# The last 448 columns of unit 28's store leave in two transfers of 123 and 5 rows

## The chip, the cores and the metric

The kernel runs on one core of one Trainium2 chip. The metric is device time in microseconds (us) of one execution, as the median of several runs. The core has TensorE (PE in the profile), VectorE (DVE), ScalarE (ACT), GpSimd (POOL) and SyncE (SP), and 16 DMA engines that carry all traffic between HBM and the on-chip memory SBUF.

## The reference

The input is `logits` of shape (32, 128, 4 heads, 4096) and `prior` of shape (32, 128, 4), both float32. Every head's row of 4096 logits goes through a softmax, the four prior values through another, and the output is the mixture of the four heads:

```
prior_probs = softmax(prior, axis=-1)                  # (32, 128, 4)
probs = softmax(logits, axis=-1)                       # (32, 128, 4, 4096)
out = sum over heads of prior_probs[..., None] * probs # (32, 128, 4096) float32
```

The logits are 268.4 MB and the output is 67.1 MB.

## The kernel before, in words

A **unit** is one of the 32 batches: 128 rows on the 128 partitions, four heads of 4096 columns each. A head of a unit is a tile of 128x4096 float32, 16 KB in each partition. The tile `ring` holds 12 of these in SBUF (L87); `place` (L101) says which of the twelve slots a head gets, so that a slot serves three units on.

The operations, one letter each in the order that is written out by hand (L26 to L60):

- `L` is `load` (L110 to L116): one transfer for a run of heads whose slots are neighbours, from `nc.sync`, that is SP.
- `M` is `peak` (L122): the negative row maximum, on VectorE. `E` is `exp` (L127): exponential and row sum on ScalarE. `R` is `recip` (L133).
- `G` is `diagonal` (L136): a 128x128 diagonal matrix of prior over row sum, on GpSimd. `X` is `weigh` (L143): TensorE multiplies by it and accumulates heads 0 to 2 in PSUM (`acc`), 512 columns an instruction.
- `C` is `weight`, `Z` is `scale`, and `A`, `B`, `T`, `V`, `P` and `W` bring head 3 and the sum in PSUM together, on VectorE (L163), or over ScalarE (L182) and GpSimd (L157, L179, L185). The result of a unit stands in the slot of its head 3, which the kernel calls `home` (L107).
- `S` is `store` (L118 to L120): it sends the result, or a stretch of its four 1024-column quarters, to HBM. Units 2 to 21 leave on ScalarE's queue, all others on SP's.

`digits` behind a letter are the head and the quarters, and `@u` is the unit. An engine runs its instructions strictly in the order in which the list gives them to it. SP therefore issues loads and stores in one row: a store whose data aren't ready holds up each load behind it.

The change concerns the end of SP's row. The last loads are those of unit 31 (`L01@31`, `L12@31`, `L23@31`, `L34@31`, one head each). Behind them SP has only stores: `S@28`, `S@29`, `S@30`, each of 128 rows of 16 KB (2048 KB), and then the four quarters of unit 31, `S23@31`, `S34@31`, `S01@31` and `S12@31`, each of 128 rows of 4 KB (512 KB). No load waits for any of these.

A transfer lies in the trace as packets, one for each row, with a start, a duration and a size, and at its end one packet of 4 bytes from each DMA engine that took part, which counts up the transfer's completion semaphore.

Of the kernel before, what the change touches and what calls it, by code (L numbers as in the profile page):

```python
# [67 lines left out]
def kernel(  # L68
# [7 lines left out]
    U, P, H, V = logits.shape  # L76
# [27 lines left out]
    def slot(u, h, a=0, b=4):  # L104
        return ring[:, place(u, h), a * C : b * C]

    def home(u, a, b):  # L107
        return slot(u, 3, a, b)
# [8 lines left out]

    def store(u, a=0, b=4):  # L118
        queue = nc.scalar if 2 <= u < 22 else nc.sync
        queue.dma_start(out=out[u, :, a * C : b * C], in_=home(u, a, b))  # L120

    def peak(u, h):  # L122
# [61 lines left out]
    def add_scaled(u, a, b):  # L184
        nc.gpsimd.tensor_add(home(u, a, b), slot(u, 1, a, b), slot(u, 3, a, b))  # L185

    step = {
        "L": load, "S": store, "M": peak, "E": exp, "R": recip, "G": diagonal, "X": weigh,
        "C": weight, "Z": scale, "A": add_last, "B": add_head, "T": add_both, "V": evac,
        "P": add_scaled, "W": add_second,  # L190
# [11 lines left out]
    with tc.manual_schedule():  # L202
# [6 lines left out]
            out=ident, in_=ident, pattern=[[-1, P]], compare_op=ALU.is_equal, fill=0.0,  # L209
# [48 lines left out]
```

## Time and profile before

| what | value |
| --- | --- |
| median of 3 runs | 787.11 us (786.59 to 787.41) |
| the profiled execution's own time | 787.09 us |
| its span, first to last instruction | 785.4 us |
| TensorE busy, share of the span | 681.8 us, 87% |
| VectorE busy | 645.1 us, 82% |
| ScalarE busy | 547.5 us, 70% |
| GpSimd busy | 293.8 us, 37% |
| moved by DMA | 335.90 MB, mean 428 GB/s |
| last instruction of VectorE (L163) starts, ends | 778.39, 779.67 us |
| `S@28`, `S@29`, `S@30` issued | 735.53, 753.93, 770.09 us |
| the four quarters of unit 31 issued | 775.15, 776.31, 777.50, 779.70 us |

The profiled execution's time is 1.69 us above its span: that is what lies around the instructions. The page of the profile gives totals, 40 slices of the span, the DMA queues and the chain of work that ended last; the view by windows gives the same shares for stretches that one chooses; the timeline gives single instructions; and the trace holds each DMA packet, without saying which of the 16 engines carried it. Queue q1 is SP's and q10 is ScalarE's; q8 and q14 carry instructions.

### The profile page before, as it was taken

The page shows a single profiled execution, that of the slowest core. Times are in us where ns is not written, and L with a number is a line of the kernel's source. Part 1 is how long each engine was busy: PE and PEld are TensorE (multiplying, and loading weights), DVE is VectorE, ACT ScalarE, POOL GpSimd, SP SyncE. Part 2 cuts the span into 40 slices and gives each one's busy share as a digit, 9 for nine tenths or more (in the row PEclk, how much of TensorE's full clock was granted, in tenths as well). Part 3 has the DMA queues.
Part 4 walks back from the last instruction along what each step waited for, and adds up shares of the span by engine and source line. Part 5 has one row for each costly group of instructions (what it writes and reads, how often), then busy time and mean ns, then how long its engine had stood idle before and what let it go on. Part 6 is the DMA issues. An engine that isn't in the chain of part 4 may idle for free.

```text
span 785.4 us, 4589 instructions
## 1 busy us (share of the span) xinstructions
PE 681.8 (87%) x1508; PEld 293.0 (37%) x1508; DVE 645.1 (82%) x327; ACT 547.5 (70%) x326; POOL 293.8 (37%) x243
## 2 busy tenths in 40 slices
PE   0959998989999888998989989898888998899996
PEld 0424433333344333433334334343333443344342
DVE  6489977897778977779877798777888887979895
ACT  2557867867668666686676776766857668779883
POOL 0033323433134332334322343323430544277892
PEclk9989999999989999999999989999989899999999
DMA  9999999999999999999999999999999999999998
GB/s 378 456 411 426 429 436 413 433 437 441 435 416 431 448 436 421 434 424 436 444 429 430 420 436 438 439 427 421 432 449 421 440 408 431 451 412 431 429 429 351
DMA packets 15335, 335.90 MB, mean 428 GB/s; under 512 B 1712, under 2 KB 1712, under 8 KB 2256
## 3 DMA queue, kind: packets, MB, share of 16 engines
q1 hardware_dynamic: 12384, 293.61, 87.1%
q10 hardware_dynamic: 2928, 42.01, 12.5%
q8 instruction: 12, 0.20, 0.1%
q14 instruction: 11, 0.09, 0.0%
HBM read 268.50 MB, written 67.11 MB: 427 GB/s over the span
## 4 chain that ended last, share of the span: by engine, by line
DMA 58%; DVE 12%; PE 10%; POOL 10%; ACT 5%; issue 4%; SPq 0%; POOLq 0%; ACTq 0%
DMA ring<-in_logits_dram 58%; DVE nmax L123 11%; PE acc L146 10%; POOL ring L185 7%; ACT ring L128 3%; ACT ring L182 2%; POOL ring L179 1%; POOL ring L157 1%; POOL diag L137 1%; DVE ring L163 0%; SPq L115 0%; DVE rden L134 0%; SPq L120 0%; POOLq L185 0%; POOLq L137 0%
## 5 line engine op out<-in xcount | busy, mean ns | idle before, releaser
L146 PE MATMUL acc<-ring,diag 128*128 128x512 f32 x1508 | 681.8, 613 | 96.6 <-ACT ring L182 62.0
L123 DVE TENSOR_REDUCE nmax<-ring 128x1 f32<-128x4096 f32 x128 | 563.0, 4409 | 114.6 <-DMA ring<-in_logits_dram 114.6
L128 ACT ACTIVATE ring<-ring,nmax 128x4096 f32<-128x4096 f32 x128 | 474.6, 3708 | 202.5 <-DVE nmax L123 202.1
L146 PEld LDWEIGHTS acc<-ring,diag 128*128 128x128 f32 x1508 | 293.0, 196 | 484.5 <-issue 358.2
L185 POOL TENSOR_TENSOR ring<-ring 128x1024 f32<-128x1024 f32 x68 | 160.1, 2374 | 20.1 <-ACT ring L182 11.2
L137 POOL TENSOR_SCALAR diag<-ident,rden,pp 128x128 f32<-128x128 f32 x96 | 43.0, 448 | 239.7 <-DVE rden L134 239.7
L153 POOL TENSOR_TENSOR wght<-rden,pp 128x1 f32<-128x1 f32 x33 | 6.3, 190 | 210.4 <-DVE rden L134 210.4
L182 ACT ACTIVATE ring<-acc 128x1024 f32<-128x1024 f32 x68 | 66.7, 1012 | 17.9 <-PE acc L146 13.8
L157 POOL TENSOR_SCALAR ring<-ring,rden,pp 128x2048 f32<-128x2048 f32 (+3 forms) x35 | 74.2, 2121 | 9.0 <-DVE rden L134 8.7
L163 DVE SCALAR_TENSOR_TENSOR ring<-ring,wght,acc 128x1024 f32<-128x1024 f32 x60 | 74.2, 1269 | 3.3 <-PE acc L146 2.3
L134 DVE RECIPROCAL rden<-dsum 128x1 f32<-128x1 f32 x128 | 19.3, 153 | 10.2 <-ACT ring L128 10.2
L128 ACT ACTIVATION_READ_ACCUMULATOR ring<-ring,nmax 128x1 f32 x128 | 24.2, 189 | 0.0
L179 POOL TENSOR_TENSOR ring<-ring 128x1024 f32<-128x1024 f32 x5 | 11.8, 2367 | 0.1
L213 DVE TENSOR_REDUCE pmax<-pr 32x128 f32<-32x512 f32 x1 | 0.7, 674 | 5.3 <-DMA pr<-in_prior_dram 5.3
L215 ACT ACTIVATE pr<-pr 32x512 f32<-32x512 f32 x1 | 0.6, 628 | 4.2 <-DVE pr L214 4.2
L163 DVE SCALAR_TENSOR_TENSOR ring<-ring,wght 128x1024 f32<-128x1024 f32 x2 | 2.5, 1280 | 0.3 <-POOL wght L153 0.3
L215 ACT ACT_TABLE_LOAD x1 | 1.3, 1283 | 1.2 <-PEq L242 1.2
L222 DVE STREAM_TRANSPOSE pp<-pn 32x128 f32<-32x128 f32 x4 | 1.2, 302 | 0.1
L216 DVE TENSOR_REDUCE pmax<-pr 32x128 f32<-32x512 f32 x1 | 0.7, 674 | 0.7 <-ACT pr L215 0.7
L218 DVE TENSOR_TENSOR pn<-pr,pmax 32x512 f32<-32x512 f32 x1 | 1.0, 1016 | 0.0
L217 DVE RECIPROCAL pmax<-pmax 32x128 f32<-32x128 f32 x1 | 0.9, 941 | 0.0
L214 DVE TENSOR_TENSOR pr<-pr,pmax 32x512 f32<-32x512 f32 x1 | 0.7, 680 | 0.0
(6 smaller groups left out, 0.9 us busy)
## 6 DMA issues: line engine op xcount, KB each, us to landing
ring<-in_logits_dram SPq DMA_DIRECT2D x27, 6144.0 KB, 34.3
ring<-in_logits_dram SPq DMA_DIRECT2D x43, 2048.0 KB, 25.5
out_dram<-ring ACTq DMA_DIRECT2D x20, 2048.0 KB, 16.1
out_dram<-ring SPq DMA_DIRECT2D x11, 2048.0 KB, 14.0
out_dram<-ring SPq DMA_DIRECT2D x4, 512.0 KB, 5.5
pr<-in_prior_dram ACTq DMA_DIRECT2D x1, 64.0 KB, 4.5
ring<-in_logits_dram SPq DMA_DIRECT2D x1, 39.5
```

Source lines behind the costliest of these rows:

```text
L123: nc.vector.tensor_reduce(out=nmax[:, u, h : h + 1], in_=slot(u, h), op=ALU.max, axis=AX.X, negate=True)
L128: nc.scalar.activation(slot(u, h), slot(u, h), AF.Exp, bias=nmax[:, u, h : h + 1], accum_out=dsum[:, u, h : h + 1],)
L134: nc.vector.reciprocal(rden[:, u, h : h + 1], dsum[:, u, h : h + 1])
L137: nc.gpsimd.tensor_scalar(out=diag[:, u % 2, h], in0=ident, scalar1=rden[:, u, h : h + 1], scalar2=pp[:, h, u : u + 1], op0=ALU.mult, op1= ...
L146: nc.tensor.matmul(acc[:, k * W : (k + 1) * W], lhsT=diag[:, u % 2, h], rhs=e[:, k * W : (k + 1) * W], start=h == 0, stop=h == H - 2 or (u ...
L153: nc.gpsimd.tensor_mul(wght[:, u, h : h + 1], rden[:, u, h : h + 1], pp[:, h, u : u + 1])
L157: nc.gpsimd.tensor_scalar(out=e, in0=e, scalar1=rden[:, u, h : h + 1], scalar2=pp[:, h, u : u + 1], op0=ALU.mult, op1=ALU.mult,)
L163: nc.vector.scalar_tensor_tensor(out=o, in0=slot(u, h, a, b), scalar=wght[:, u, h : h + 1], in1=more, op0=ALU.mult, op1=ALU.add,)
L179: nc.gpsimd.tensor_add(e, e, slot(u, 2, a, b))
L182: nc.scalar.activation(slot(u, 1, a, b), acc[:, a * C : b * C], AF.Copy)
L185: nc.gpsimd.tensor_add(home(u, a, b), slot(u, 1, a, b), slot(u, 3, a, b))
L215: nc.scalar.activation(pr, pr, AF.Exp)
```

## The change

For unit 28 alone, `store` issues three transfers where it issued one, all on SP and at the same place in the order: first all 128 rows with the columns 0 to 3647, then rows 0 to 122 with the last 448 columns, then rows 123 to 127 with the last 448 columns. The bytes are the same. A row of the first is 14592 B, one of the other two is 1792 B (they were 16384 B in one).

```
     def store(u, a=0, b=4):
         queue = nc.scalar if 2 <= u < 22 else nc.sync
+        if u == U - 4:
+
+            o, c = home(u, a, b), V - 448
+            for p, q, i, j in ((0, P, 0, c), (0, 123, c, V), (123, P, c, V)):
+                queue.dma_start(out=out[u, p:q, i:j], in_=o[p:q, i:j])
+            return
         queue.dma_start(out=out[u, :, a * C : b * C], in_=home(u, a, b))
```

No other instruction is added, removed or moved; lines below `store` have numbers that are 6 higher.

## The prediction

> **What bounds the kernel.** I read the page's slices and queues first: are the DMA engines ever idle?
>
> ```profile
> DMA  9999999999999999999999999999999999999998
> ...
> q1 hardware_dynamic: 12384, 293.61, 87.1%
> q10 hardware_dynamic: 2928, 42.01, 12.5%
> ```
>
> The 16 engines are at 90% or more in 39 of 40 slices, and two queues fill 99.6% of 16 engines' span. All else has gaps (TensorE 87%). So DMA time counts, and the question is what ends last on it. Next, the view by windows of the last 20 us (columns: PE, PEld, DVE, ACT, POOL, clock, DMA share, GB/s).
>
> ```profile
> 765.00:770.00 5.00, 4.86 (x12) 1.92 (x11) 4.54 (x4) 4.30 (x3) 5.00 (x3) 1.00 1.01 433
> 770.00:775.00 5.00, 5.00 (x13) 2.28 (x12) 3.92 (x4) 3.30 (x2) 0.82 (x4) 1.00 1.00 426
> 775.00:780.00 5.00, 3.36 (x8) 1.14 (x6) 3.75 (x4) 0.00 (x0) 0.00 (x0) 1.00 0.96 399
> 780.00:785.40 5.40, 0.00 (x0) 0.00 (x0) 0.00 (x0) 0.00 (x0) 0.00 (x0) 0.80 0.43 174
> ```
>
> The engines are full to 775, nearly full to 780, and then 43% busy on average over the last 5.4 us, in which nothing computes. Some are done early, and some work to the end. The chain of waits stops at the last VectorE instruction and the timeline shows SP's stores:
>
> ```profile
> 767.79 10.58 PE acc L146 x24
> 778.37 0.03 issue
> 778.39 1.28 DVE ring L163
> ```
>
> ```profile
> 735.53 44.50 SPq L120 DMA_DIRECT2D out_dram<-ring  x7
> ```
>
> The last quarter is ready at 779.67 and issued at 779.70. The packet records show the rest. An engine starts its next packet 3 to 4 ns before the last one ends, so the records can be sorted into 16 gapless chains; each then holds the same 774 packets of q1 and 183 of q10. The instant at which each chain finished its part of `S@29`, in order:
>
> 772.30, 772.56, 772.58, 772.76, 772.82, 772.96, 773.18 | 773.47, 774.01, 774.18, 774.36, 774.52 | 774.63, 775.04, 775.41, 775.51
>
> From there each has the same work: 8 rows of 16 KB and 32 of 4 KB. The median step from one packet to the next is 607 ns for 16 KB and 155 ns for 4 KB: 8 x 0.607 + 32 x 0.155 = 9.82 us, and with five closing packets 9.86. The latest chain: 775.51 + 9.86 = 785.37, the end of the span. It never waits. The early chains do: seven were idle when the last quarter came, took it up at 781.94 to 782.16 and ended near 783.3. **So the end is the backlog of the latest chain**, 2.1 us behind what compute allows. The four latest chains are those that carried two of the twelve 16 KB instruction packets of q8 (about 1.0 us each); no other carried more than one.
>
> **The change, part by part.** Nothing that computes is touched. Work moves between chains. `S@28` lies in the backlog: issued at 735.53, its packets run from 762.6 to 770.6.
>
> *Row prices.* The trace of before has no store row of 14592 or 1792 B. The line through the two store rows is 155 + (607 - 155) x (B - 4096) / 12288: 541 ns for 14592 B, 70 ns for 1792 B. Bounds for 1792 B: 66 ns at the 16 KB row's rate, and 155 ns, were it no cheaper than a 4 KB row. The nearest row, a 2 KB load row of the prior, took 84 ns, a step of 80. I take 70, since 66 and 80 stand near it.
>
> *Every chain* sends 8 shorter rows: 8 x (607 - 541) = 0.53 us less.
>
> *The 123 rows.* All recorded transfers go out in equal shares: 128 rows as 8 on each of 16, the prior's 32 rows as 2 on each. 123 is 3 x 41, so the largest number of engines up to 16 that can take equal shares is 3: 41 x 70 ns = 2.87 us on each of three. The 5 rows go to five engines, 0.07 us each. The sum: three chains +2.87 + 0.07 + 0.01 - 0.53 = **+2.42 us**, two chains -0.45, the others **-0.53**. Bounds: 41 x 66 gives +2.26, 41 x 155 gives +5.9.
>
> The Trainium skill states this rule: in "DMA: Bandwidth & Descriptors", "Why a DMA increments its semaphore by 16 and not by 1", a transfer from SP runs on the largest number up to 16 that divides its outermost dimension, on the lowest-numbered engines. By that rule too it is 3 and 5 engines; the trace of before agrees with 16 for 128 and for 32 rows, and has no case with fewer, nor numbers of engines.
>
> *Two more issues on SP.* A large issue took 0.33 to 0.42 us. Each transfer takes one of eight completion semaphores in turn and waits until its last user has landed. The 123-row part so waits for a load that landed at 736.4, the 5-row part for one that landed at 741.3. Behind them on SP is `S@29`, issued only at 753.93 because GpSimd released it; both are gone by then, and their rows' turn comes at 762 or later. The four quarters then wait for older transfers, landed by 771 at the latest; they were issued from 775. Cost nothing; without that cover, 0.8 us.
>
> The same page of the Trainium skill, under "Rules for kernel authors", speaks against the change: transfers under 64 KB pay mostly overhead. The 5 rows are 9 KB. By its estimate of a fixed 2.0 us per transfer the two pieces would add 4 us if they stood alone at the end; the trace shows the store queued 27 us ahead of its packets, so I count none of it.
>
> *Sum.* The new end is 785.37 plus the larger of -0.53 (latest chain, if spared) and (x + 2.42 - 775.51), x being the latest of the three loaded chains. No gain is left from x = 773.09 on. What is late next is one of the three.
>
> *Which chains?* The trace doesn't number engines. Two rows speak to it, if a transfer is handed to engines in a fixed order. The last quarter was picked up first by the chains of 773.18, 772.58, 772.82 and 772.96 (781.94 to 781.99 us). The first load was picked up first by those of 772.96, 774.36 and 773.18 (3.211 to 3.218), and the latest four only as 10th, 12th, 13th and 14th. I take the first reading, though only early chains could show in it, because two of its chains lead in both. Then x is 772.96 or 773.18, and the end moves by -0.13 to +0.09. The time is the profiled 787.09 - 0.1 = **787.0 us** (that run is 0.02 below the median).
>
> **The rivals.**
> 1. *Middle chains loaded* (x from 773.47 to 774.52): +0.38 to +1.43, so 787.5 to 788.5. The first load's order speaks for it (774.36: +1.27, 788.4). At 80 ns a row even the forecast's chains would give +0.5.
> 2. *Slower: one of the four latest is loaded* (x from 774.63): +1.54 to +2.42, so 788.6 to 789.5. It decides from x = 774.66. For it: 4 of 16 chains, and three drawn blindly would contain one in 1 - (12 x 11 x 10) / (16 x 15 x 14) = 61%. Against it: all four are picked up late in the first load, and none is seen early anywhere.
> 3. *It doesn't do what it says:* 123 rows spread over 16 as 7 or 8 each. Per chain 8 x 541 + 9 x 70 against 8 x 607: +0.1, 787.2. Nothing recorded has unequal shares.
> 4. *Dearer:* all 123 rows on one engine, 8.61 us: +4.9 to +8.2, 792.0 to 795.2; or 155 ns a row, x = 773.18 + 5.9: +3.6, 790.7. No row supports either.
>
> **How the numbers follow.** Forecast 0.48, rival 1 0.20, rival 2 0.23, rival 3 0.04, rival 4 0.05. What a measurement can tell from no change is about 0.2%, 1.57 us. The largest gain that the sum allows is 0.53 us (0.07%), so "faster" has only the 0.02 for scatter between runs, taken from the forecast. Same: 0.46 + 0.20 + 0.04 = 0.70, and slower 0.23 + 0.05 = 0.28. The forecast's own range is 786.4 (all three earliest, -0.53, and 0.2 of scatter) to 787.2. The whole range must reach to rival 2, whose likeliest value is its top: 786.4 to 789.5.
>
> **What would show it.** Each step can be read from the packets of the changed kernel: 8 rows of 14592 B near 541 ns on each chain, 41 of 1792 B near 70 ns on three chains and one on each of five; an issue of the 5 rows near 741 with `S@29` still at 754; `S@29` landing on the three chains 2.42 us later than without, on the latest ones 0.53 earlier. I am wrong if the loaded chains are among the latest, if the 1792 B row costs over 80 ns, if the shares aren't 41, or if the backlog of the latest chain isn't the same from one execution to the next, which one trace can't show.

## The result, and the profile after

The median is 787.93 us over 20 runs (787.64 to 788.77) against 786.84 us over 20 runs of the kernel before (786.50 to 787.76). The ratio is 1.0013 with a 95% interval of 1.0007 to 1.0019: the change makes the kernel **slower by about 1.0 us** (0.6 to 1.5). The profiled execution took 787.82 us, with a span of 786.1 us against 785.4.

That is 0.13%, less than the 0.2% that the prediction took as the bound of what can be told; with 20 runs on each side it can be told.

The first question is whether any engine computes later than before. This is the end of the chain of waits of the changed kernel:

```profile
767.74 10.58 PE acc L152 x24
778.32 0.03 issue
778.35 1.28 DVE ring L169
```

The last VectorE instruction starts at 778.35; before it was 778.39. Nothing that computes is late, so the 0.7 us of span came behind it. The view by windows of the changed kernel (PE, PEld, DVE, ACT, POOL, clock, DMA share, GB/s) has the same columns as the one of before:

```profile
765.00:770.00 5.00, 4.86 (x13) 1.88 (x12) 4.48 (x4) 4.36 (x3) 5.00 (x4) 1.00 1.00 422
770.00:775.00 5.00, 5.00 (x13) 2.27 (x12) 3.97 (x5) 3.25 (x2) 0.78 (x4) 1.00 0.98 416
775.00:780.00 5.00, 3.31 (x8) 1.14 (x6) 3.71 (x4) 0.00 (x0) 0.00 (x0) 1.00 0.95 392
780.00:786.10 6.10, 0.00 (x0) 0.00 (x0) 0.00 (x0) 0.00 (x0) 0.00 (x0) 0.65 0.37 152
```

DMA moves a little less in each stretch and the last one is longer at a lower share: 0.37 of 6.10 us, where it was 0.43 of 5.40. Multiplied out, that is 2.26 us of all engines against 2.32. The same work is spread less evenly: more engines are done early and a few work longer.

SP's own view: its timeline from 738 us, where the first line is the 5 rows and the second `S@29` (start, duration), and the new row of its waits.

```profile
740.34 11.21 SPq L124 DMA_DIRECT2D out_dram<-ring  x1
753.85 0.37 SPq L126 DMA_DIRECT2D out_dram<-ring  x1
```

```profile
SPq L124 <- DMA ring<-in_logits_dram: 3.9, 1, 3.9
```

The wait of 3.9 us is the foreseen one, for an older load. The issue of the 5 rows wasn't: SP was busy with it for 11.21 us, where an issue had taken 0.33 to 0.42. It was over at 751.55, and `S@29` went out at 753.85 (753.93 before), as soon as it was ready. So the added issues and their wait held nothing up, with 2.3 us to spare.

The packet records, sorted into 16 gapless chains as in the prediction, show where the time went. First, their clock: the prediction set the packets' times so that the last packet ends with the span, at 785.37. On the profile's own clock the last packet of the kernel before ends at 783.96, its completion is counted at 784.30, and DMA moves nothing in the last 1.40 us:

```profile
784.00:785.40 1.40, 0.00 (x0) 0.00 (x0) 0.00 (x0) 0.00 (x0) 0.00 (x0) 0.50 0.00 0
```

So every packet time of the prediction is 1.40 us late against the instructions' times. In the changed kernel the last packet ends at 784.75, 1.34 us ahead of the end of the span. The packet times below, of the experiments too, are set as in the prediction, last packet at the end of the span, so that they can be compared with it; differences between chains of one trace don't depend on that, and between the kernel before and the change it makes 0.06 us.

For each chain: when its part of `S@29` ended, the rows of 1792 B that it carried, and its instruction packets (16 KB and 8 KB, by the microsecond of their start).

```
        after                                       |  before
 ends    small rows  16 KB      8 KB                |  ends    16 KB      8 KB
776.24   41 + 1      -          122 327 535 737     | 774.01   -          120 327 533 737
775.54   41 + 1      -          150 411 668         | 773.47   -          150 412 668
774.85   -           68 566     -                   | 775.41   68 566     -
774.73   -           128 626    -                   | 775.04   130 627    -
774.28   -           199 692    -                   | 775.51   199 692    -
773.95   -           256 754    -                   | 774.63   253 754    -
773.82   41 + 1      -          -                   |   one of 772.30 to 772.82, no packets
```

The instruction packets come at the same times in both, so they serve as names for the chains. Three chains carry 42 small rows. The latest of them ended 775.51 - 774.01 = 1.50 us ahead of the latest chain before. Its main rows took 4.34 us and its small ones 2.97, 7.32 us with the closing packets where one store had taken 4.86: 2.46 us more. It now ends last: 776.24 + 9.86 = 786.10, or 784.75 on the profile's clock, 0.79 us later than the last packet of the kernel before (783.96). Behind it lie the same 1.3 to 1.4 us without DMA.

### The profile page after: what moved, and what is told of

Read it like the earlier page. It is cut to its first block, busy times and chain, and to the rows that moved or that the text cites. A ratio compares the mean times of both kernels' runs of the same rounds, so it can differ in the third digit from the quotient of the medians.

```text
span 786.1 us, 4590 instructions
## 1 busy us (share of the span) xinstructions
PE 679.6 (86%) x1508; PEld 292.1 (37%) x1508; DVE 645.3 (82%) x327; ACT 547.2 (70%) x326; POOL 293.8 (37%) x243
## 4 chain that ended last, share of the span: by engine, by line
DMA 58%; DVE 12%; PE 10%; POOL 10%; ACT 5%; issue 4%; SPq 0%; POOLq 0%; ACTq 0%
DMA ring<-in_logits_dram 58%; DVE nmax L129 11%; PE acc L152 10%; POOL ring L191 7%; ACT ring L134 3%; ACT ring L188 2%; POOL ring L185 1%; POOL ring L163 1%; POOL diag L143 1%; DVE ring L169 0%; SPq L115 0%; DVE rden L140 0%; SPq L126 0%; POOLq L191 0%; POOLq L143 0%
```

## The experiments

The theory after the result is that of **unequal shares**: three chains carry 41 rows each, and the end is the backlog of the latest of these, which lay in the middle before. The rivals: the two added **issues** cost, the long one above all, or the **small rows** cost by themselves, however they are shared. The edits below stand for the tuple in the loop of `store`, with `c = V - 448` unless given.

**Equal shares, three transfers.**

```
for p, q, i, j in ((0, P, 0, c), (0, P, c, c + 224), (0, P, c + 224, V)):
```

> Unit 28's store still goes out in three transfers on SP, but all three have 128 rows (columns 0 to 3647, then twice 224 columns), so all 16 chains get equal shares. Theory of shares (what costs is that three chains carry 41 rows each): each chain has 8 rows of 14592 B at 541 ns and 16 of 896 B at 37 ns, 4.93 us instead of 4.86, so +0.1 us against the kernel before. Rival of issues (the two added transfers cost by being issued, waited for and closed, whoever carries them): the same +1 us as the change.

Measured: 787.01 against 787.00 us, ratio 1.0001 (0.9993 to 1.0010). The number of issues is that of the change, 256 rows are even half as long, and nothing is lost. Small rows and the number of issues are out as causes; but no issue was long here (0.46 us at most), so the long one is left for the next run.

**The two small transfers in the other order.**

```
for p, q, i, j in ((0, P, 0, c), (123, P, c, V), (0, 123, c, V)):
```

> The change with its two small transfers in the other order, 5 rows and then 123. In the change, SP spent 11.21 us on the issue of the 5 rows behind the 123 (740.34 to 751.55), against 0.33 us in the run with equal shares. If an issue is held while the queue of one engine that it uses is too full, the 5-row issue now takes about 0.35 us, and the next issue to meet the full queues is that of unit 29's store, at 753.9, when they have drained: no issue over 1 us. If instead it is the 123-row transfer that SP is still busy with, its own issue or the next one takes 11 us again. By the theory of unequal shares the time is that of the change in both cases, +1.0 us (+0.5 to +1.5), since the shares are the same; were the held issue the cause of the loss, it would be gone: 0.

Measured: 787.91 against 787.05 us, +0.9, ratio 1.0010 (1.0001 to 1.0019): the loss of the change. SP's timeline from 738 us, the issue of the 123 rows and that of `S@29`:

```profile
739.87 0.26 SPq L124 DMA_DIRECT2D out_dram<-ring  x1
753.41 0.36 SPq L126 DMA_DIRECT2D out_dram<-ring  x1
```

The long issue is gone and the time is not better; the chain that ends last is again one with 42 small rows, at 776.34 for its part of `S@29`. So the long issue wasn't the cause, and it belongs to a transfer that is issued soon behind the 123 rows.

**Double the columns.**

```
o, c = home(u, a, b), V - 896
```

> The change with 896 columns in place of 448. Theory of shares: the 1792 B rows become 3584 B at 136 ns, 41 x 136 = 5.58 us, the main rows give back 1.06, one row of the five adds 0.15, so +4.67 us on three chains; if the latest of these is the one that ended at 774.01 before, it ends 778.68 - 775.51 = 3.2 us later than the latest chain of before: +3.2 us. Were it an early chain (773.2), +2.4; were it the latest, +4.7. Rival of issues: +1 us as in the change, since the number of transfers is the same.

Measured: 790.18 against 787.00 us, +3.2, ratio 1.0042 (1.0028 to 1.0055). In the trace the chain with the packets at 120, 327, 535 and 737 is last again: its part of `S@29` ends at 778.79, where 778.68 was worked out. The last VectorE instruction of this kernel starts at 777.81, earlier than before, so all of it is backlog.

**Fewer columns.**

```
o, c = home(u, a, b), V - 192
```

> The change with 192 columns in place of 448. Theory of shares: 768 B rows at 32 ns, 41 x 32 = 1.33 us, the main rows give back 0.23, so +1.15 us on three chains; with the latest of them at 774.01 it ends at 775.16, the spared latest chain at 775.28: -0.2 us, within what can be measured. Rival of issues: +1 us.

Measured: 787.00 against 787.00 us, ratio 1.0001 (0.9992 to 1.0010); span 785.3. The loss is gone with the same three transfers and the same 3 engines. The expected gain of 0.2 is too small to be told from none. The long issue of the 5 rows is still there, which is a second sign that it costs nothing:

```profile
740.59 10.96 SPq L124 DMA_DIRECT2D out_dram<-ring  x1
```

**127 and 1 rows.**

```
for p, q, i, j in ((0, P, 0, c), (0, 127, c, V), (127, P, c, V)):
```

> The change with 127 and 1 rows in place of 123 and 5. Theory of equal shares: 127 is prime, so all 127 rows of 1792 B go to one engine, 127 x 70 ns = 8.89 us, and the one row too: +8.4 us on one chain with the main rows' 0.53 given back. That chain is one of the three that the change loaded: had it ended at 774.01 without, +6.9 us; at 773.47, +6.4; at 772.3 to 772.8 (the one without instruction packets), +5.2 to +5.7. Rival (rows are spread over all engines that are free, and the change's loss has another cause): +1 us or less.

Measured: 791.78 against 787.14 us, +4.6, ratio 1.0060 (1.0046 to 1.0074). One chain carries all 127 rows and the one row; its part of `S@29` ends at 779.73. It is a chain without instruction packets, the earliest kind, so the loss is smaller than 8.4 us. The two last windows of this kernel:

```profile
780.00:785.00 5.00, 0.00 (x0) 0.00 (x0) 0.00 (x0) 0.00 (x0) 0.00 (x0) 0.65 0.49 201
785.00:789.60 4.60, 0.00 (x0) 0.00 (x0) 0.00 (x0) 0.00 (x0) 0.00 (x0) 0.50 0.04 18
```

One engine of 16 busy for the whole 4.60 us would be a share of 0.0625; 0.04 is one engine for some 3 us, and then the stretch without DMA: the whole core waits for one. The expected loss was 5.2 to 5.7, so +4.6 missed it; 779.73 less the 8.4 is 771.3, so this chain stood a microsecond earlier than its kind in the trace of before. SP's timeline from 740 us:

```profile
740.51 24.19 SPq L124 DMA_DIRECT2D out_dram<-ring  x1
764.79 1.44 SPq L126 DMA_DIRECT2D out_dram<-ring  x1
```

Here the issue behind the many rows lasts 24.19 us, and `S@29` goes out 11 us late. Eight chains stand idle for 0.4 to 2.8 us for it, which the late chain doesn't feel.

**125 and 3 rows.**

```
for p, q, i, j in ((0, P, 0, c), (0, 125, c, V), (125, P, c, V)):
```

> The change with 125 and 3 rows in place of 123 and 5. Theory of equal shares: 125 is 5 x 25, so five chains take 25 rows each, 1.75 us, three of them one more, and all give back 0.53: +1.2 to +1.3 us. The five are the three loaded by the change and the two that carried one row there; the latest of them ended at 774.5 without, so 775.8 against 775.5: +0.3 us, a third of the change's loss, and the trace shows five chains with 25 or 26 rows. Rival (it is the small rows or the partitions they lie in that cost, not how many engines share them): +1 us as in the change, since the 57 KB are the same.

Measured: 787.50 against 787.14 us, +0.4, ratio 1.0006 (0.9997 to 1.0015). Five chains carry 25 rows, three of them one more; they are the five that had small rows in the change. The median is where the theory puts it, but the interval reaches from -0.2 to +1.2 us, so the time alone doesn't decide against the rival's +1. Its trace speaks for the theory: the latest of the five ends its part of `S@29` at 775.71, where 775.8 was expected, and the span is 785.6, between 785.4 and 786.1.

**The last 448 columns left out.** This kernel doesn't write those columns of unit 28.

```
for p, q, i, j in ((0, P, 0, c),):
```

> Leaves out the last 448 columns of unit 28: the store has only its 128 rows of 14592 B, and the output lacks those columns. Theory of backlog: every chain gives back 8 x 66 ns, so the end comes 0.5 us earlier, -0.5 us (0.07%). Rival (the end is set by when the last quarter is computed, and the stores behind it take a fixed time): 0 us.

Measured: 786.60 against 786.99 us, -0.4, ratio 0.9992 (0.9983 to 1.0001). The median agrees with the backlog's -0.5; the interval just reaches no change, so it isn't shown by this run alone.

**The same split at unit 24.**

```
if u == U - 8:
```

> The change's split, for unit 24's store in place of unit 28's: some 110 us before the end, with the loads of seven more units behind it on the same queue. Theory of backlog: no chain is idle between there and the last stores, so the three chains keep their 2.4 us to the end as if they had got it at unit 28: +0.7 to +1.1 us, like the change. Rivals: the lag is worn off because loads wait for free slots in between (0 us); or every later load lands later and the computing engines lose the time too (+2 us or more).

Measured: 789.15 against 786.99 us, +2.2, ratio 1.0026 (1.0017 to 1.0035). The expectation of backlog alone failed here; the second rival holds. The last line of VectorE's timeline, of this kernel:

```profile
780.11 1.28 DVE L169 SCALAR_TENSOR_TENSOR ring<-ring,wght,acc 128x1024 f32<-128x1024 f32 x1 [0.93 <-PE acc L152]
```

It starts 1.7 us later than in the kernel before, so here the computing engines are late too. SP's waits between 635 and 700 us, first of this kernel and then of the one before (total, times, longest):

```profile
SPq L115 <- DMA out_dram<-ring: 30.3, 2, 15.8
```

```profile
SPq L115 <- DMA out_dram<-ring: 26.4, 2, 13.2
```

A load waits for the store that frees its slots, and a store has landed only when its slowest chain is done. The first load so held up is issued at 654.11 instead of 652.77, and the issues from 677 us on stay 0.9 to 1.7 us late. At unit 28 no load stands behind the split.

**Whole rows, 112, 8 and 8.**

```
for p, q, i, j in ((0, 112, 0, V), (112, 120, 0, V), (120, P, 0, V)):
```

> Unit 28's store in three transfers of whole rows: 112 rows (7 on each of 16 chains), then 8 rows and 8 rows. By equal shares the two small ones go to the same eight engines, the first of the numbering, one 16 KB row each time. Theory of shares: eight chains +0.62 us, eight -0.61; if none of the four latest chains is among the first eight, the end is the larger of 774.90 and 774.52 + 0.62 = 775.14, so -0.4 us; if one of them is, +0.6. Rival of issues: +1 us.

Measured: 789.96 against 787.00 us, +3.0, ratio 1.0041 (1.0028 to 1.0054). None of the theories had this. The shares are as expected: eight chains have one row in each of the small transfers, and none of the four latest is among them. But rows of 16 KB, 0.611 us elsewhere, took up to 3.30 us here. Two windows of this kernel, and then the same two of the kernel before:

```profile
765.00:768.00 3.00, 2.95 (x7) 0.95 (x5) 3.00 (x3) 2.59 (x1) 3.00 (x4) 1.00 1.13 360
768.00:772.00 4.00, 3.89 (x9) 1.82 (x10) 3.27 (x4) 3.42 (x3) 2.96 (x4) 1.00 0.89 324
```

```profile
765.00:768.00 3.00, 2.86 (x8) 1.08 (x7) 3.00 (x3) 2.89 (x1) 3.00 (x3) 1.00 1.00 426
768.00:772.00 4.00, 4.00 (x10) 1.79 (x10) 3.29 (x4) 3.42 (x3) 2.64 (x3) 1.00 1.01 430
```

Over the two windows the engines are as busy as before (1.13 and then 0.89; the view counts a packet whole in the window in which it starts) but move 360 and 324 GB/s instead of 426 and 430: busy is not moving.

**Whole rows, 112 and 16.**

```
for p, q, i, j in ((0, 112, 0, V), (112, P, 0, V)):
```

> Unit 28's store in two transfers of whole rows, 112 and 16. Both can be shared equally by 16 engines, so each chain has 8 rows of 16 KB as in the kernel before. If the +3 us of the run with 112, 8 and 8 rows came from the unequal shares, this run shows no change (0 us) and rows of 611 ns. If it came from rows that several engines read at once out of neighbouring partitions (packets of up to 3.3 us there), such packets show here too, and the end is +1 to +4 us.

Measured: 790.07 against 787.14 us, +2.9, ratio 1.0036 (1.0022 to 1.0050). Shares are equal and the loss is there, with 25 packets of 16 KB above 0.7 us in the last 30 us and the longest at 1.79 (35 such in the run above, none in the kernel before). So it isn't the shares. The expectation's other idea, several engines on neighbouring partitions at once, was not tested by itself: the trace doesn't say which rows an engine carried. The cause stays open.

**A version meant to gain: 119 and 9 rows of 384 columns.**

```
o, c = home(u, a, b), V - 384
for p, q, i, j in ((0, P, 0, c), (0, 119, c, V), (119, P, c, V)):
```

> A version meant to gain: the last 384 columns in transfers of 119 and 9 rows. Theory of equal shares: 119 is 7 x 17, so seven chains take 17 rows of 1536 B at 61 ns, 1.04 us, nine take one row more, and all give back 0.45 on the main rows: +0.65 us on seven, -0.4 on the others. The run with 112, 8 and 8 rows put its extra rows on none of the four latest chains, and seven is less than eight; so the latest of the seven ends at 774.52 + 0.65 = 775.17, the latest of the rest at 775.1, and the end moves by -0.3 to -0.4 us, at the edge of what can be measured; the trace can show it by chains. If one of the latest were among the seven, +0.65. Rival (any such split costs): +0.5 us or more.

Measured: 786.92 against 787.14 us, ratio 0.9999 (0.9990 to 1.0007). Seven chains carry 17 rows and one more, none of them one of the four latest; the latest chain ends `S@29` at 775.31, 0.2 earlier than before. No loss, and no gain that can be told.

**The kernel before, a second trace.**

> The kernel before again, for a second trace of it. If the order of the 16 chains is fixed by the program, the four with two 16 KB instruction packets are the latest again, near 775.5 at the end of unit 29's store, and the chain with four 8 KB instruction packets ends near 774.0. If it changes from one execution to the next, other chains are latest.

Measured: 787.10 us, span 785.4. The four chains with two 16 KB instruction packets are the latest again (774.96 to 775.53), and the chain with the packets at 121, 325, 534 and 737 ends at 774.60, not 774.01. The order by kind is much the same in the two traces; a single chain moves by some 0.6 us between executions. In the run with equal shares one of the four, at 774.25, even ends ahead of two chains with 8 KB packets only (774.34 and 774.40).

## Why the prediction was wrong

The predicted 787.0 us stood for no loss (-0.13 to +0.09); the measured ratio excludes that. The time lies in the range and is that of rival 1, 787.5 to 788.5, which had a chance of 0.20.

- *What bounds the end: right, but not to the end of the span.* The latest chain's backlog sets it. Computing ended at the same time in the change, and with 896 columns the end followed the loaded chain to 0.2 us. But that chain doesn't end with the span, as the prediction had it: its last packet lies 1.40 us ahead of it. The sums go by differences, so they stand.
- *Row prices: right.* A row of 1792 B takes 74 ns, 70.8 from one to the next (70 predicted), and a main row 545 ns, 542 from one to the next (541).
- *Shares: right.* Three chains with 41 rows, five with one; and 127, 125 and 119 rows went to 1, 5 and 7 chains. The rule of the Trainium skill that the prediction named ("DMA: Bandwidth & Descriptors", "Why a DMA increments its semaphore by 16 and not by 1") agrees with each of these counts. The lowest-numbered engines it names fit too, as far as a trace without numbers can tell: the chain of the 127 rows is of the kind without instruction packets, as one of the three is, and the five of 125 rows include the three.
- *The sum on a loaded chain: right.* +2.46 us measured, +2.42 predicted.
- *Two more issues on SP: right in the sum, wrong in the size.* They cost nothing, and the wait is there. But they weren't 0.8 us: the second took 11.21. The cover, `S@29` not being ready before 753.85, was 2.3 us from being used up. The fixed 2.0 us per transfer that the prediction took from the Trainium skill, "DMA: Bandwidth & Descriptors", is a fit for transfers issued from GpSimd; here, on SP and behind a backlog, three transfers with equal shares took no longer than one (787.01 against 787.00 us).
- *"Which chains?": wrong, and this is the step that failed.* The prediction took x as 772.96 or 773.18, from the order in which chains picked up a newly issued transfer. The chains that were loaded are those of 774.01, 773.47 and one of 772.30 to 772.82. In the changed kernel they picked up the first load as 9th or 13th, as 8th, and as 3rd, 5th or 10th of 16; in the first 22 us packets of two chains end within the same nanosecond more than a dozen times, so a chain can't always be followed back to its first packet. So the order of pick-up didn't show the numbering. The reading that was preferred was also biased: only chains that are idle can be first to pick up the last quarter, and only early chains are idle. Nor can it be read from the records, since chains are told apart by the overlap of their packets, and a chain that was idle has none. Without it the forecast had little: three chains drawn blindly would all be among the seven earliest in (7 x 6 x 5) / (16 x 15 x 14) = 6%, where the prediction gave 0.48. With x = 774.01 the same sum gives 775.51 + 0.92, and 787.09 + 0.92 = 788.0 us, against 787.93 measured. That it agrees to 0.1 is partly luck, since that one chain moves by 0.6 us between executions.
- *The bound of 0.2%* was too wide for this kernel with 20 runs each: 0.13% stands clear of noise here.
- *Rival 2 and its price* didn't happen: none of the four latest chains was loaded, in any of these runs.

Left open: the trace doesn't say why the loaded chain of the 127 rows stood at 771.3 (in the trace of the change, the three other chains without instruction packets ended at 770.89 to 771.70, which is 771.4 to 772.2 with the main rows' 0.53 put back), or how much of the spread among runs of the changed kernel (787.64 to 788.77) is the movement of that one chain.

## What to carry to other kernels

When the DMA engines have a backlog to the end, as here, the time is that of the latest single engine, not of the mean: sort the packets into one chain per engine and look at each one's slack. Set the packets against the instructions by the trace's own clock, not by the end of the span. A transfer whose row count has no large divisor up to 16 puts its rows on few engines (127 rows on 1, 123 on 3, 125 on 5, 119 on 7); that may fill slack, but only if one knows which engines these are, and a short experiment (127 rows, then look which chain carries them) told it here where the reading of start times didn't. The same split in front of loads cost twice as much (+2.2 us against +1.0), with loads that waited longer for stores to land (30.3 us against 26.4).

## What the runs showed of the hardware that was not expected

- 128 rows of 16 KB sent as 112 and 16, or 112, 8 and 8, took up to 1.79 and 3.30 us a row where 0.611 is usual, and cost 2.9 and 3.0 us, though each engine's number of rows changed by one at most. The cause is open.
- The issue of a transfer behind one that puts many rows on few engines keeps SP busy: 11.21 us behind 41 rows on each of three, 2.87 behind 25 on each of five, 24.19 behind 127 on one, under 0.5 behind 17 on seven or 8 on sixteen. It is as long behind 41 rows of 768 B (10.96) and of 3584 B (11.84), so it doesn't go by the bytes. On the profile's clock it ended when the fullest chain had some 73 packets still to start in the first case, as many in the second, and some 125 in the third; which limit that is stays open.
- The instruction packets lie unevenly on the DMA engines, in the kernel before: four chains carry two 16 KB packets of about 1 us, four one, four only 8 KB packets of 0.31 us, and four none. The 3.2 us between the earliest and the latest chain go largely by these kinds, again so in the second trace of before; that the packets cause them was not tested by itself.
